# Two more column pairs of a decoder trunk with shared forms of x, further split pairs, and splits kept in order

## The chip, the cores and the metric

The kernel runs on one core of one Trainium2 chip. The metric is device time in microseconds (us), the median of the runs shown. The core's engines go by the profile's short names: PE (TensorE's matrix multiplications), PEld (its weight loads), DVE (VectorE), ACT (ScalarE), POOL (GpSimd) and SP (SyncE, which here only issues DMAs). Each engine works through a queue of its own in a fixed order and waits for the others by semaphores.

## The reference

One layer of a hybrid decoder for 256 tokens and a model width of 2048. All is float32.

```python
h = rmsnorm(x, norm_mix_g)
u = h @ w_in                     # 2048 x 12288
c_g, b_g, xa, za, q, fl, iv, og, ga, gb = split(u)   # 8 fields of 1024 columns, 2 of 2048
ya = b_g * causal_dwconv3(c_g * xa, conv_w) * silu(za)
o  = hgrn2_chunked(silu(q), (1 - lb) * sigmoid(-fl), iv, log_f(fl))   # gated recurrence, 8 heads of 128
yb = rmsnorm_per_head(o) * hg_norm_g * silu(og)
m  = sigmoid(ga) * (ya @ w_a_out) + sigmoid(gb) * (yb @ w_b_out)
x  = x + m @ w_o
x  = x + sigmoid(rmsnorm(x, ple_norm_g) @ w_ple_gate) * (p @ w_ple_proj)
return rmsnorm(x, final_norm_g)
```

## The kernel before

**Products.** Each float32 operand is split into a rounded high part and the rest: ACT writes the high part (`whi`, L154), DVE subtracts it from the operand for the low part (`wlo`, L155). A product of 128 rows by 128 tokens by 512 columns is then three matmuls: high by high, high by low, low by high. The norm's gain is folded into the transposed x when that is split (`put`, L258); the norm's factor for each token (`rstd1`) is applied when a result leaves PSUM.

**Groups and steps.** The columns of each weight are cut into groups of 512, and a group into chunks of 256 rows; a chunk is one step of the main loop. The groups follow one another: four for p (`PP`), then the fields of `w_in` in `IN_ORDER` (L37): for each half j of 512 columns f, q, iv, og, c, xa, za, b, then the gates with A (`w_a_out`) and B (`w_b_out`), then O (`w_o`) and PG (`w_ple_gate`). An ordinary step has 12 matmuls: two parts of 128 rows, two halves of 128 tokens, three matmuls each. The result lies in two PSUM banks, one for each half of the tokens.

**Pairs.** Three groups "GG" take the columns of a gate ga and a gate gb together, and "GP" two of the last gate's, in an order written out as a program (`GATES`, `LATE`, L42). An entry (g, c) is two ordinary steps of group g. An entry ("S", c) is the same chunk of both groups at once: a scheme with 7 in place of 8 products, in four steps of 2, 1, 2 and 2 products (`pair_products`, L1166). It needs combinations of the four weight blocks, made in place by DVE (`combine_weights`, L162 to L170: one operation of 1024 columns, two of 512, with a new tile `t2`), and four combinations of x, its forms (`forms`, L729, fed by `forms_of_x`, L750, which loads x anew). Its products are added into banks named 1, 5, 6, 7 (tag "s") and (0, 0), (1, 0), (0, 1) (tag "g", a half of the tokens and a group of the pair); `sums` (L773) adds these up, with one ACT copy and seven DVE additions, as soon as they are complete. The four steps split the weights as ordinary steps do, the second one half of a tile.

**Banks.** PSUM has eight banks here, four with the tag "g" and four with "s" (`bank`, L89). A bank that is asked for while its four are in use waits until one has been read.

**What goes ahead.** At each step the loop first splits the weights for the steps up to `ahead(pos)` in front (`ahead`, L1147; the loop at L1228): three, and one more around the GG groups. The split pairs lie in four buffers of the pool `wp`; around the GG groups one more pair in `tmp2` takes every fifth step (`more`, L214; `MORE`, L209). Weights come in units of two chunks, 1 MB, into three buffers `raw` (`load`, L103); `ask_ahead` (L1158) asks for them on SP's queue, in that queue's order with all other transfers.

**Epilogues.** What is done with a result is a generator; `advance` lets each active one do its next part after a step, behind the last splits (`step`, L1129, through `issue_after`, which sets the order in an engine's queue). Some results are turned by way of DRAM (`turned`, L292): four stores, a load, a 32 by 32 transposition on DVE. When the kernel is built, instructions get their places in the engines' queues by an assumed duration of each, with program order as the priority.

**Around the change.** Step 4 is f's first (half 0). At steps 10 to 13 x is loaded by tokens (`load_tokens`, L1042), at 13 to 16 ACT sums its squares (L1050), at 16 the norm's factor follows (`norm_of_x`, L1054: DVE, then POOL at L278), and at step 17 `ep_f` (L348) begins: ACT reads f's two banks (`scaled`, L315). Until then f keeps these two banks. q follows at step 12 and iv at step 20. `ep_q` (L399) makes q times its sigmoid and turns it, `ep_iv` (L405) scales the value, `ep_og` (L411) makes the output gate and then runs the recurrence (`hgrn`, L419), whose tiles X, a, both, aoff, y lie in `tmp1` and, for part of X, in the place of `ybT`. Temporaries of 4 KB a partition come from eight buffers (`t4`, L85).

Of the kernel before, what the change touches and what calls it, by code (L numbers as in the profile page):

```python
# [15 lines left out]
P = 128  # L16
# [7 lines left out]
CW = 512  # L24
# [17 lines left out]
GATES = ("S", 0), (0, 2), ("S", 1), (1, 2), ("S", 4), (0, 6), ("S", 5), (1, 6)  # L42
LATE = (0, 4), ("S", 0), (0, 6), ("S", 1), (2, 3), ("S", 2), (1, 4), (1, 6)
# [8 lines left out]
def hybrid_kernel(ctx, tc, xT, x, pT, prm, gfin, masks, w_in, w_a, w_b, w_o, w_pg, w_pp, out):  # L52
# [80 lines left out]
    def split(pos, c0=0, c1=2 * CW):  # L133
# [9 lines left out]
        if more(pos) and pos % (4 + MORE) < MORE:  # L143
            pool, n = pools[more(pos)], MORE
        if pos not in parts:
            parts[pos] = tuple(
                pool.tile([P, 2 * CW], F32R, tag=tag, bufs=n, name=nm(tag)) for tag in ("whi", "wlo")
            )
        hi, lo = parts[pos]
        s = slice(c0, c1)  # L150
        with ExitStack() as order:
            for i in state["before"].pop() if state.get("before") else ():
                order.enter_context(tc.issue_after(i))
# [8 lines left out]
    def combine_weights(pos):  # L162

        b = load(pos).rearrange("p i (k c) -> p (i k) c", k=2)
        t2 = half[unit_of[pos]] = pools["tmp2" if pos in gates else "tmp3"].tile([P, CW], F32, tag="t2", bufs=2 if pos in gates else 1, name=nm("t2"))
# [8 lines left out]
    for n, (kind, j) in enumerate(IN_ORDER):  # L174
        if j == 0 or kind not in ("ga", "gb"):
# [33 lines left out]
    LEAD, MORE = 3, 1  # L209
    of_kind = lambda *kinds: [pos for pos, (gi, c) in enumerate(steps) if groups[gi][0] in kinds]  # L210
    gates, late = of_kind("GG"), of_kind("PG")[0]
    gates = range(gates[0] - 12, gates[-1] + 9)

    def more(pos):  # L214

        return "tmp2" if pos in gates else None

    TOKENS, NORM = 10, 13
# [186 lines left out]
    def ep_iv(j, psum):  # L405
        v = t4("v", 1)
# [322 lines left out]
    def forms(op, pool, tag, r, chunks):  # L729
# [12 lines left out]
        hi, lo = (pool.tile([P, 4 * n * P], F32R, tag=tag + x, bufs=1, name=nm(tag + x)) for x in "hl")  # L742
# [7 lines left out]
    def forms_of_x():  # L750

        joined = sorted(c for u, c in GATES if u == "S")
        for n in range(0, len(joined), 2):
# [11 lines left out]
            yield from forms("hT", pools["tmp2"], f"Sx{n}", r, chunks)  # L765
# [35 lines left out]
    def ep_pair(j, e, left):  # L801
# [12 lines left out]
        yield from sums(e, left, tiles_of, then)  # L814

# [28 lines left out]
    def ep_o(j, psum):  # L844
# [18 lines left out]
        if j < 2:  # L863
# [9 lines left out]
            yield from forms("x1T", pools["tmp3"], f"So{j}", r, chunks)  # L873
# [273 lines left out]
    def ahead(pos):  # L1147

        return LEAD + min(max(pos - late - 4, 0) // 3, 5) + MORE * (more(pos + LEAD) is not None and more(pos + LEAD + MORE) == more(pos + LEAD))
# [67 lines left out]
    for pos, (gi, c) in enumerate(steps[:last_group]):  # L1217
# [26 lines left out]
        if pos == 4:  # L1244
            begin()
        if 0 <= pos - NORM < 4:
# [7 lines left out]
        if program:  # L1254
# [4 lines left out]
            if c == (min(n for n, (u, _) in enumerate(program) if u == "S"), 0):  # L1259
                active.append({"GG": ep_pair, "GP": ep_gates_late}[kind](j, banks, left))  # L1260
            pair_products(c, program, opname)
            ask_ahead()
            if not joint[pos] or c[1] % 2:
# [150 lines left out]
```

## Time and profile before

| | |
|---|---|
| runs, us | 814.44, 814.02, 814.43; median 814.43 |
| profiled execution | 814.02 us, of which the profile's span is 812.2 |
| mean granted TensorE clock | 0.996 |
| PE busy | 802.9 us, 4199 matmuls |
| PEld busy | 667.5 us |
| DVE busy | 625.9 us, 737 instructions |
| ACT busy | 463.5 us, 607 instructions |
| POOL busy | 91.1 us |
| DMA | 188.33 MB, mean 232 GB/s |

A matmul's record overlaps that of the next, so PE's busy time is how long at least one was under way, and the pace is read from the starts. In a list of groups the two numbers behind the bar are the busy time of the group in us and the mean of one in ns, and behind the next bar stands the idle time of the engine just ahead of these instructions with what ended it. In a timeline or a chain the first number is the start, the second the time it took.

### The profile page before, as it was taken

To read this page: it belongs to the slowest core of one execution; us is meant where nothing else is said; L and a number is where in the kernel's file an instruction comes from. 1 tells how busy PE (TensorE), PEld (TensorE's weight loads), DVE (VectorE), ACT (ScalarE), POOL (GpSimd) and SP (SyncE) were. 2 spreads that over 40 slices of the span, in tenths; PEclk is the share of its full clock that TensorE was granted. 3 is DMA by queue.
4 is the path that set the end of the run, shared out by engine and by line. 5 is a ranking of instruction groups with operands and counts; after the bars stand their busy time and mean duration, and the time that the engine had idled before them with its cause. 6 is when DMAs were issued, how large, how long until landed. Compare 5 with 4: busy or idle time off the path is not lost.

```text
span 812.2 us, 10984 instructions
## 1 busy us (share of the span) xinstructions
PE 802.9 (99%) x4199; PEld 667.5 (82%) x4199; DVE 625.9 (77%) x737; ACT 463.5 (57%) x607; POOL 91.1 (11%) x74
## 2 busy tenths in 40 slices
PE   9999999999999999999999999999999999999995
PEld 7888888888888888888888888888888888888885
DVE  5747697967766488967767998998997657679895
ACT  7667465555555465565664554564564456665652
POOL 1000045400000055200001000100100000002012
PEclk9999999999999999999999999999999999999998
DMA  9979656747767555647764774774866687887542
GB/s 339 372 276 342 224 170 208 230 167 238 257 234 255 184 185 201 214 155 261 271 239 146 225 268 148 250 258 157 259 230 230 215 304 245 295 301 270 201 144 105
DMA packets 46565, 188.33 MB, mean 232 GB/s; under 512 B 5296, under 2 KB 14768, under 8 KB 31408
## 3 DMA queue, kind: packets, MB, share of 16 engines
q1 hardware_dynamic: 46368, 187.36, 67.5%
q8 instruction: 33, 0.54, 0.3%
q10 hardware_dynamic: 144, 0.26, 0.1%
q14 instruction: 20, 0.16, 0.1%
HBM read 173.97 MB, written 13.63 MB: 231 GB/s over the span
## 4 chain that ended last, share of the span: by engine, by line
PE 88%; DVE 5%; DMA 3%; ACT 1%; issue 1%; SPq 0%; POOL 0%; ACTq 0%; POOLq 0%; DVEq 0%
PE g L1156 70%; PE g L1178 11%; PE s L1178 4%; DMA raw<-in_w_pg 2%; DVE wlo L155 2%; PE s L1156 1%; PE s L457 1%; ACT whi L154 1%; DVE raw L166 1%; DMA raw<-in_w_pp 0%; DVE t L920 0%; DVE xs L921 0%; DMA turn<-t 0%; DVE t L169 0%; DVE t L938 0%
## 5 line engine op out<-in xcount | busy, mean ns | idle before, releaser
L155 DVE TENSOR_TENSOR wlo<-raw,whi 128x1024 fp32r<-128x1024 f32 (+1 forms) x310 | 384.4, 1255 | 156.3 <-ACT whi L154 154.9
L154 ACT ACTIVATE whi<-raw 128x1024 fp32r<-128x1024 f32 (+1 forms) x310 | 320.0, 1049 | 250.7 <-PE g L1156 197.4
L1156 PE MATMUL g<-wlo,xh 128*128 128x512 f32 (+1 forms) x656 | 251.9, 384 | 0.0
L1156 PE MATMUL g<-whi,xl 128*128 128x512 f32 (+1 forms) x656 | 251.7, 384 | 0.0
L1156 PE MATMUL g<-whi,xh 128*128 128x512 f32 (+1 forms) x656 | 251.6, 385 | 0.0
L1156 PEld LDWEIGHTS g<-whi,xh 128*128 128x128 f32 x656 | 123.3, 188 | 24.5
L1156 PEld LDWEIGHTS g<-whi,xl 128*128 128x128 f32 x656 | 123.3, 188 | 24.5
L1156 PEld LDWEIGHTS g<-wlo,xh 128*128 128x128 f32 x656 | 123.3, 188 | 24.0
L1178 PE MATMUL g<-wlo,xh 128*128 128x512 f32 x166 | 64.6, 389 | 0.0
L1178 PE MATMUL g<-whi,xl 128*128 128x512 f32 x166 | 64.6, 389 | 0.0
L1178 PE MATMUL g<-whi,xh 128*128 128x512 f32 x166 | 64.4, 389 | 0.0
L1156 PE MATMUL g<-whi,mh 128*128 128x512 f32 x128 | 49.8, 389 | 0.0
L1156 PE MATMUL g<-wlo,mh 128*128 128x512 f32 x128 | 49.8, 389 | 0.0
L1156 PE MATMUL g<-whi,ml 128*128 128x512 f32 x128 | 49.6, 389 | 0.0
L154 ACT ACTIVATE whi<-t 128x512 fp32r<-128x512 f32 x15 | 9.5, 632 | 54.4 <-DVE t L169 54.4
L1178 PEld LDWEIGHTS g<-whi,xl 128*128 128x128 f32 x166 | 31.2, 188 | 6.5
L1178 PEld LDWEIGHTS g<-whi,xh 128*128 128x128 f32 x166 | 31.2, 188 | 6.5
L1178 PEld LDWEIGHTS g<-wlo,xh 128*128 128x128 f32 x166 | 31.1, 188 | 6.4
L832 POOL TENSOR_TENSOR t<-ga,gb 128x512 f32<-128x512 f32 x6 | 10.6, 1786 | 192.9 <-issue 118.1
L1156 PEld LDWEIGHTS g<-whi,ml 128*128 128x128 f32 x128 | 24.0, 188 | 5.0
L1156 PEld LDWEIGHTS g<-wlo,mh 128*128 128x128 f32 x128 | 24.0, 188 | 5.0
L1156 PE MATMUL g<-whi,yaTh 128*128 128x512 f32 (+1 forms) x74 | 28.0, 385 | 0.1
(250 smaller groups left out, 919.8 us busy)
## 6 DMA issues: line engine op xcount, KB each, us to landing
raw<-in_w_in SPq DMA_DIRECT2D x73, 1024.0 KB, 5.0
raw<-in_w_in SPq DMA_DIRECT2D x34, 512.0 KB, 6.6
raw<-in_w_o SPq DMA_DIRECT2D x16, 1024.0 KB, 6.0
raw<-in_w_pg SPq DMA_DIRECT2D x12, 1024.0 KB, 6.4
turn<-t SPq DMA_DIRECT2D x72, 128.0 KB, 2.7
t<-turn SPq DMA_DIRECT2D x18, 512.0 KB, 5.4
raw<-in_w_a SPq DMA_DIRECT2D x8, 1024.0 KB, 5.2
raw<-in_w_b SPq DMA_DIRECT2D x8, 1024.0 KB, 5.3
```

The lines of the kernel that those rows point to most:

```text
L154: a = nc.scalar.activation(out=hi[:, s], in_=src[:, s], func=AF.Copy)
L155: v = nc.vector.tensor_tensor(out=lo[:, s], in0=src[:, s], in1=hi[:, s].bitcast(F32), op=ALU.subtract)
L166: nc.vector.tensor_tensor(out=b[:, 0:4:3, :], in0=b[:, 0:3:2, :], in1=b[:, 3:4, :].to_broadcast([P, 2, CW]), op=ALU.subtract)
L457: nc.tensor.matmul(heads(bk)[r, h, c if at is None else slice(at, at + 32)], key(h)[:, r], query(h)[:, c], start=True, stop=True, tile_pos ...
L832: (nc.vector if j == 3 else nc.gpsimd).tensor_tensor(out=spread(m, t), in0=blocks(ga[:, s]), in1=blocks(gb[:, s]), op=ALU.add)
L1156: nc.tensor.matmul(psum, a, b, start=first and n == 0, stop=last and n == 2)
L1178: nc.tensor.matmul(banks[name], x, y[:, s], start=k == total[name] and i == 0, stop=k == 1 and i == 2)
```

## The change

q and iv of half 0 become one pair ("QV"), iv and og of half 1 another ("VG"). Both follow a new program, `INNER`: two ordinary entries of the first group, an S, one more of the first group, an S, then three of the second group. So half 0 has f, QV, og, c and so on, and half 1 f, q, VG, c. A new epilogue `ep_inner` adds the banks up by `sums` and hands the two results, now in SBUF, to the epilogues that they had before; `ep_iv` scales in place.

The forms of x for chunks 0 and 1 are made for these pairs too, from a load at step 9 (`FORMS`), into the part of `yaT` that half 1 fills later. Around the two pairs three steps of seven have their split pair in other tiles: both buffers of X; a and y; the two later parts of `ybT`. There up to three more steps are split ahead. The tile `t2` lies in `both` or `aoff`. And every split in the kernel is put behind the split before it in the queues of ACT and DVE (`state["splits"]`).

```diff
--- before.py
+++ after.py
@@ -40,6 +40,7 @@
 
 
 GATES = ("S", 0), (0, 2), ("S", 1), (1, 2), ("S", 4), (0, 6), ("S", 5), (1, 6)
+INNER = (0, 2), (0, 4), ("S", 0), (0, 6), ("S", 1), (1, 2), (1, 4), (1, 6)
 LATE = (0, 4), ("S", 0), (0, 6), ("S", 1), (2, 3), ("S", 2), (1, 4), (1, 6)
 
 
@@ -140,16 +141,18 @@
                 src, c1 = half[unit_of[pos]], CW
 
         pool, n = (pools["late"], 6) if (pos - state.get("late", len(steps))) % 10 < 6 and "late" in state else (wp, 4)
-        if more(pos) and pos % (4 + MORE) < MORE:
-            pool, n = pools[more(pos)], MORE
+        places = [(pool, n, tag) for tag in ("whi", "wlo")]
+        n = len(MORE[more(pos)])
+        if pos % (4 + n) < n:
+            places = [(pools[name], 1 + (tag == "X"), tag) for name, tag in MORE[more(pos)][pos % (4 + n)]]
         if pos not in parts:
             parts[pos] = tuple(
-                pool.tile([P, 2 * CW], F32R, tag=tag, bufs=n, name=nm(tag)) for tag in ("whi", "wlo")
+                pool.tile([P, 2 * CW], F32R, tag=tag, bufs=n, name=nm("w" + x)) for (pool, n, tag), x in zip(places, ("hi", "lo"))
             )
         hi, lo = parts[pos]
         s = slice(c0, c1)
         with ExitStack() as order:
-            for i in state["before"].pop() if state.get("before") else ():
+            for i in (*state.get("splits", ()), *(state["before"].pop() if state.get("before") else ())):
                 order.enter_context(tc.issue_after(i))
             a = nc.scalar.activation(out=hi[:, s], in_=src[:, s], func=AF.Copy)
             v = nc.vector.tensor_tensor(
@@ -162,7 +165,10 @@
     def combine_weights(pos):
 
         b = load(pos).rearrange("p i (k c) -> p (i k) c", k=2)
-        t2 = half[unit_of[pos]] = pools["tmp2" if pos in gates else "tmp3"].tile([P, CW], F32, tag="t2", bufs=2 if pos in gates else 1, name=nm("t2"))
+        pool, tag, n = ("tmp2", "t2", 2) if pos in gates else ("tmp3", "t2", 1)
+        if more(pos) == "inner":
+            pool, tag, n = "tmp1", ("both", "aoff")[unit_of[pos] // 2 % 2], 1
+        t2 = half[unit_of[pos]] = pools[pool].tile([P, CW], F32, tag=tag, bufs=n, name=nm("t2"))
         nc.vector.tensor_tensor(
             out=b[:, 0:4:3, :], in0=b[:, 0:3:2, :], in1=b[:, 3:4, :].to_broadcast([P, 2, CW]), op=ALU.subtract
         )
@@ -172,7 +178,11 @@
     groups = []
     groups += [("PP", j, w_pp, j, "pT") for j in range(4)]
     for n, (kind, j) in enumerate(IN_ORDER):
-        if j == 0 or kind not in ("ga", "gb"):
+        if (kind, j) in (("q", 0), ("iv", 1)):
+            groups.append(("QV" if j == 0 else "VG", j, w_in, n, "hT", INNER))
+        elif (kind, j) in (("iv", 0), ("og", 1)):
+            continue
+        elif j == 0 or kind not in ("ga", "gb"):
             groups.append((kind, j, w_in, n, "hT"))
         elif kind == "ga":
             groups.append(("GG", j, w_in, n, "hT", GATES))
@@ -206,16 +216,25 @@
     last_group = len(steps) - w_pg.shape[2]
 
 
-    LEAD, MORE = 3, 1
+
+    LEAD = 3
+    MORE = {
+        None: (), "gates": ((("tmp2", "whi"), ("tmp2", "wlo")),),
+        "inner": (
+            (("tmp1", "X"), ("tmp1", "X")), (("tmp1", "a"), ("tmp1", "y")), (("branch", "ybTh1"), ("branch", "ybTl1")),
+        ),
+    }
     of_kind = lambda *kinds: [pos for pos, (gi, c) in enumerate(steps) if groups[gi][0] in kinds]
     gates, late = of_kind("GG"), of_kind("PG")[0]
     gates = range(gates[0] - 12, gates[-1] + 9)
+    inner = [of_kind(kind) for kind in ("QV", "VG")]
+    inner = range(inner[0][0] - 3, inner[0][-1] + 1), range(inner[1][0] - 6, inner[1][-1] + 1)
 
     def more(pos):
 
-        return "tmp2" if pos in gates else None
-
-    TOKENS, NORM = 10, 13
+        return "gates" if pos in gates else "inner" if any(pos in at for at in inner) else None
+
+    TOKENS, NORM, FORMS = 10, 13, 9
     FIRST = 6
 
     praw = t4()[:, : 2 * T]
@@ -402,8 +421,8 @@
         plain_times(psum, sg, qt)
         state["qT", j] = yield from turned(qt, 5, t4("qT", 1))
 
-    def ep_iv(j, psum):
-        v = t4("v", 1)
+    def ep_iv(j, psum, v=None):
+        v = t4("v", 1) if v is None else v
         scaled(psum, v)
         state["v", j] = v
         yield
@@ -726,7 +745,7 @@
         yield
 
 
-    def forms(op, pool, tag, r, chunks):
+    def forms(op, made, r, chunks):
 
 
         n = len(chunks)
@@ -739,7 +758,7 @@
         nc.vector.tensor_tensor(out=s3, in0=a11, in1=a21, op=ALU.subtract)
         nc.vector.tensor_tensor(out=s4, in0=a12, in1=s2, op=ALU.subtract)
         yield
-        hi, lo = (pool.tile([P, 4 * n * P], F32R, tag=tag + x, bufs=1, name=nm(tag + x)) for x in "hl")
+        hi, lo = made()
         nc.scalar.activation(out=hi, in_=f, func=AF.Copy)
         nc.vector.tensor_tensor(out=lo, in0=f, in1=hi.bitcast(F32), op=ALU.subtract)
         for u in range(n):
@@ -747,9 +766,13 @@
                 s = slice((n * i + u) * P, (n * i + u + 1) * P)
                 state["S", op, chunks[u], i] = hi[:, s], lo[:, s]
 
-    def forms_of_x():
-
-        joined = sorted(c for u, c in GATES if u == "S")
+    def form_tiles(pool, tag, n=2):
+
+        return lambda: tuple(pool.tile([P, 4 * n * P], F32R, tag=tag + x, bufs=1, name=nm(tag + x)) for x in "hl")
+
+    def forms_of_x(program, made):
+
+        joined = sorted(c for u, c in program if u == "S")
         for n in range(0, len(joined), 2):
             chunks = joined[n : n + 2]
             raw = t4()
@@ -762,7 +785,7 @@
                     h = r[:, u, k, :]
                     nc.scalar.activation(out=h, in_=h, func=AF.Identity, scale=gain(PRM_GMIX, 2 * chunks[u] + k))
             yield
-            yield from forms("hT", pools["tmp2"], f"Sx{n}", r, chunks)
+            yield from forms("hT", made(n), r, chunks)
             yield
 
     def add(out, x, y):
@@ -812,6 +835,16 @@
                 )
 
         yield from sums(e, left, tiles_of, then)
+
+    def ep_inner(j, e, left):
+
+        def then(q, g):
+            halves = [g[:, A], g[:, B]]
+            after = ep_iv(j, halves, g) if q != j else (ep_og if j else ep_q)(j, halves)
+            next(after)
+            active.append(after)
+
+        yield from sums(e, left, lambda: (t4("v", 1), t4()) if j else (t4(), t4("v", 1)), then)
 
     def ep_a(j, psum):
         g = state["ga", j]
@@ -870,7 +903,7 @@
             yield
             chunks = [c for u, c in LATE if u == "S" and c // 2 == j]
             r = x1.rearrange("p (u k t) -> p u k t", u=2, k=2)[:, : len(chunks)]
-            yield from forms("x1T", pools["tmp3"], f"So{j}", r, chunks)
+            yield from forms("x1T", form_tiles(pools["tmp3"], f"So{j}", len(chunks)), r, chunks)
             return
         for c in range(4):
             put(state["x1T"], j * 4 + c, x1[:, c * T : (c + 1) * T], gain(PRM_GPLE, j * 4 + c))
@@ -1146,7 +1179,10 @@
 
     def ahead(pos):
 
-        return LEAD + min(max(pos - late - 4, 0) // 3, 5) + MORE * (more(pos + LEAD) is not None and more(pos + LEAD + MORE) == more(pos + LEAD))
+        at, n = more(pos + LEAD), 0
+        while n < len(MORE[at]) and more(pos + LEAD + n + 1) == at and (at == "gates" or more(pos + LEAD - 2 * n) == at):
+            n += 1
+        return LEAD + min(max(pos - late - 4, 0) // 3, 5) + n
 
     def product(psum, op, k, t, hi, lo, first, last, which=(0, 1, 2)):
 
@@ -1243,6 +1279,10 @@
             load_x(pos + 2)
         if pos == 4:
             begin()
+        if pos == FORMS:
+            held = [x[:, 4:, :].rearrange("p k t -> p (k t)") for x in state["yaT"]]
+            active.append(forms_of_x(INNER, lambda n: lambda: held))
+            step(active[-1])
         if 0 <= pos - NORM < 4:
             add_squares(pos - NORM)
         if pos == NORM + 3:
@@ -1257,9 +1297,11 @@
                 total = products_of(program)
                 left, banks = dict(total), {}
             if c == (min(n for n, (u, _) in enumerate(program) if u == "S"), 0):
-                active.append({"GG": ep_pair, "GP": ep_gates_late}[kind](j, banks, left))
+                active.append({"GG": ep_pair, "GP": ep_gates_late, "QV": ep_inner, "VG": ep_inner}[kind](j, banks, left))
             pair_products(c, program, opname)
             ask_ahead()
+            if 0 <= pos - TOKENS < 4:
+                load_tokens(pos - TOKENS)
             if not joint[pos] or c[1] % 2:
                 advance()
             if kind == "GP" and c in ((1, 1), (3, 1)):
@@ -1304,7 +1346,7 @@
             if kind == "ga" and j == 0:
                 finish()
                 second_part()
-                active.append(forms_of_x())
+                active.append(forms_of_x(GATES, lambda n: form_tiles(pools["tmp2"], f"Sx{n}")))
                 step(active[-1])
             if kind == "O" and j == 0:
                 state["x1T"] = operand(big, "x", KT)
```

## The prediction, made before the result was known

> **What bounds the kernel now.** I read the page first: the busy times, then the slices.
>
> ```profile
> span 812.2 us, 10984 instructions
> ...
> PE 802.9 (99%) x4199; PEld 667.5 (82%) x4199; DVE 625.9 (77%) x737; ACT 463.5 (57%) x607; POOL 91.1 (11%) x74
> ...
> PE   9999999999999999999999999999999999999995
> ...
> PEclk9999999999999999999999999999999999999998
> DMA  9979656747767555647764774774866687887542
> ```
>
> PE is busy in every slice but the last, at full clock. DVE comes next with 77%, and DMA is nearly full in the first four slices, some 80 us. Busy alone doesn't say that PE is never late, so I went to the chain of work that ended last, whose PE pieces give the true pace:
>
> ```profile
> 16.36 119.68 PE g L1156 x528
> ...
> 178.21 138.73 PE g L1156 x612
> ```
>
> 119.68/528 and 138.73/612 are both 0.2267 us a matmul: stretches of 120 us and more without a hole. The 384 ns that the page gives as the mean of one overlap their neighbours, so a matmul that goes away is worth 0.2267 us, not 0.384. The forecast has one main term then: how many matmuls go. And one question: does PE stay as dense?
>
> The Trainium skill, "TensorE: Matmul & The Clock Gate", section "Back-to-back issue gap", gives about 131 ns sustained for 512 columns; by that twelve matmuls would be an estimated 1.6 us. The trace shows 0.2267 us here, and it decides.
>
> **The change part by part.**
>
> *Matmuls removed.* A plain unit of two chunks takes 2 x 12 matmuls, and a joint unit ("S") of four steps 6+3+6+6 = 21. Each program of INNER has two S units, and two pairs use it: 4 x 3 = 12 matmuls go, 12 x 0.2267 = **2.72 us**. They lie in stretches where PE is dense, so all of it counts if nothing stalls. Nothing else leaves PE.
>
> *Vector and scalar work added.* From the groups by line:
>
> ```profile
> L155 DVE TENSOR_TENSOR wlo<-raw,whi 128x1024 fp32r<-128x1024 f32 (+1 forms) x310 | 384.4, 1255 | 156.3 <-ACT whi L154 154.9
> L154 ACT ACTIVATE whi<-raw 128x1024 fp32r<-128x1024 f32 (+1 forms) x310 | 320.0, 1049 | 250.7 <-PE g L1156 197.4 <-issue 13.8 <-DMA raw<-in_w_pg 12.3
> L166 DVE TENSOR_TENSOR raw<-raw 128x1024 f32<-128x1024 f32 x15 | 19.3, 1289 | 0.4
> L169 DVE TENSOR_TENSOR t<-raw 128x512 f32<-128x512 f32 x15 | 11.4, 757 | 0.5
> L170 DVE TENSOR_TENSOR raw<-raw,t 128x512 f32<-128x512 f32 x15 | 10.4, 692 | 0.5
> L155 DVE TENSOR_TENSOR wlo<-t,whi 128x512 fp32r<-128x512 f32 x15 | 10.4, 691 | 0.7
> L769 DVE TENSOR_TENSOR gb<-gb,s 128x512 f32<-128x512 f32 (+1 forms) x9 | 7.7, 861 | 0.0
> L769 DVE TENSOR_TENSOR ga<-gb,g 128x512 f32<-128x512 f32 x6 | 4.1, 682 | 0.0
> L769 DVE TENSOR_TENSOR gb<-gb,g 128x512 f32<-128x512 f32 x6 | 3.8, 684 | 0.0
> ```
>
> An S unit costs DVE 3 x 1.255 + 0.691 + 1.289 + 0.757 + 0.692 = 7.2 us where a plain unit costs 2.5: +4.7, four times 18.8. The sums of a pair are a third of the three L769 groups, (7.7+4.1+3.8)/3 = 5.2, twice 10.4. The forms of x once: about 1.6 for four quarter-size operations, an estimate from the 0.69 of half-size ones, and 1.25 for the low part, which has the shape of a full split. Together 32 us, so DVE goes from 626 to about 658 of 810 us (81%). ACT gets some 11 us (four full and four half splits are 6.3 by its row; the rest copies and the scaling of x). None is on PE's path while splits are made ahead. In an S unit DVE needs 7.2 us against 21 x 0.2267 = 4.8 of PE, so the lead must be there beforehand: over one program DVE's splits take 6 x 2.5 + 2 x 7.2 = 29.4 us and PE 186 x 0.2267 = 42.2. The three added split pairs let splits run six steps ahead instead of three: up to 16 us of cover in plain steps, against a deficit of 2.4 us an S unit. If the cover were gone, those 2.4 us would be the price of each. The windows say where DVE has room:
>
> ```profile
> 27.00:38.00 11.00, 11.00 (x51) 9.09 (x50) 8.47 (x12) 5.64 (x7) 0.00 (x0) 1.00 1.01 378
> 38.00:49.00 11.00, 11.00 (x50) 9.13 (x49) 4.91 (x4) 5.28 (x6) 0.00 (x0) 1.00 1.03 412
> 60.00:71.00 11.00, 11.00 (x50) 9.13 (x49) 7.34 (x7) 6.08 (x8) 0.00 (x0) 1.00 0.99 305
> 71.00:82.00 11.00, 11.00 (x50) 9.09 (x50) 8.81 (x14) 9.97 (x13) 0.00 (x0) 1.00 0.95 359
> 257.00:268.00 11.00, 11.00 (x50) 9.13 (x49) 5.81 (x5) 5.50 (x6) 0.00 (x0) 1.00 0.54 179
> ```
>
> (Columns: the stretch and its length, then busy PE, PEld, DVE, ACT, POOL with counts, the clock, DMA share, GB/s.) The second pair, around 240 to 284 us, has half of DVE and DMA free: I cost it at nothing beyond its gain of 1.36 us. The query's sums, gates and turned copy end some 5 us later than now, but their reader, the recurrence, starts after og at 103 us, 20 us on.
>
> *DMA added and moved.* Two loads of 256 KB of x at step 9, about 30 us in, on the full DMA: 0.52 MB at 378 to 412 GB/s is 1.3 us of delay for what queues behind on SP: weights, then the four loads of x by tokens. The weight loads are asked for as far ahead as the splits, so three steps earlier against the turned copies, for which SP stands still; that helps and is costed at nothing.
>
> *The bank that the first pair needs earlier.* Only four banks have the tag "g". The first group, f0, holds two until its eviction at L315, since that needs the norm of x, which needs the tokens:
>
> ```profile
> L1046 SPq DMA_DIRECT2D t<-in_x x4: 328/380/496, 33.9 to 41.3; - x4
> ...
> DMA to landing us min/median/max: 8.4/9.9/10.2
> ```
>
> ```profile
> 55.44 1.04 ACT L1050 ACTIVATE t<-t 128x1024 f32<-128x1024 f32 x1
> ...
> 57.90 1.27 ACT L315 ACTIVATE t<-g,r1r 128x512 f32<-128x512 f32 x2 [1.32 <-POOL r1r L278]
> ```
>
> ```profile
> 59.71 0.39 PE L1156 MATMUL g<-whi,xh 128*128 128x512 f32 x1
> ```
>
> The first eviction ends at 57.90 + 0.69 = 58.6, the second at 59.2; the value's first matmul, at 59.71, takes the fifth bank: half a microsecond to spare. In the changed kernel the fifth bank is (0, 1), first written in the last part of the first S unit. The query starts at 16.36 + 96 x 0.2267 = 38.1; four plain steps and 15 matmuls later is 38.1 + 63 x 0.2267 = **52.4 us**. The eviction cannot be that early: the last token load, issued at 41.3, lands by 51.5 at the latest and then 1.3 later, at 52.8; from the last square's start to the first eviction's end it takes 58.6 - 55.44 = 3.15. So the bank is free at 55.9 at the earliest, 3.5 us after PE would want it. Unmoved it is 6.2; with the squares behind the second S unit's combinations on DVE (2.7 us more) 8.9. That is the unknown of this change: 0 to 8.9.
>
> What lies beside that wait is other matmuls. The matmuls' order is fixed when the kernel is built, and the trace shows that it isn't always the program's:
>
> ```profile
> 734.32 0.61 PE L1178 MATMUL g<-whi,xh 128*128 128x512 f32 x2
> ...
> 736.13 0.39 PE L1156 MATMUL g<-whi,xh 128*128 128x512 f32 x1
> ...
> 737.04 0.39 PE L1178 MATMUL g<-whi,xl 128*128 128x512 f32 x1
> ```
>
> Here the gate's first group (L1156) lacks its last part of x1, and matmuls of the next pair (L1178) stand in between, without a hole. In the same way three matmuls of the S unit (0.7 us) and the 24 of (0, 6) on banks already held (5.4 us) can go ahead of bank (0, 1): 6.1 us, about the 6.2 needed. What stands behind a matmul that waits is all of PE, so what isn't covered counts in full. I take the wait as nearly hidden: 0.1 by these numbers, **0.3 us** with some allowance. The ends stay 0 and 8.9 less what is filled.
>
> *Splits in order of use; other buffers.* Each split is put behind the one before it on ACT and DVE. With a shared order nothing is issued more. It can lose where a split waits for its buffer ahead of one that needn't. ACT's largest wait in its row above is for PE's release, which comes in order of use as well: 0, within plus or minus 0.5. The tiles borrowed for splits (X, a, y and others) are first written by the recurrence about a step after the pair ends: 0.
>
> *Sum.* The profiled execution took 814.02 us (span 812.2 and 1.8 around it). 814.02 - 2.72 + 0.3 = 811.6. The runs shown have a median of 814.43, 0.4 above it; I go half way: **811.8**.
>
> **The rivals.**
>
> *Part of the wait stays.* The order is fixed before, by assumed durations; where norm and eviction come later on the chip than assumed, PE stands. The chain from the last square to the eviction crosses four engines, which speaks for it. 2 us left, a third of the 6.2, gives 814.02 - 2.72 + 2 = 813.3. The same place and size would fit the forms of x, or the first S unit's splits, coming late.
>
> *The wait stays whole (the other side).* If no matmul is put ahead, PE stands from 52.4 to about 58.6: 814.02 - 2.72 + 6.2 = 817.5. It turns slower than before when more than 2.7 us stay uncovered. For it speaks that the program has (0, 1) first; against it the interleaving above. A clock drop could follow:
>
> ```profile
> 800.00:805.00 5.00, 3.79 (x32) 3.59 (x30) 3.52 (x12) 2.17 (x4) 0.62 (x2) 1.00 0.55 210
> 805.00:812.00 7.00, 0.00 (x0) 0.00 (x0) 2.14 (x6) 1.33 (x2) 0.54 (x1) 0.57 0.39 150
> ```
>
> PE's last work ends at 803.8; a mean of 0.57 over 7 us is full clock for 1 us and half for 6, so it fell 2.2 us after. How soon it returns no row shows: between 0 and the 6 us seen, at half pace 0 to 3 us, so up to 820.5. The Trainium skill, "TensorE: Matmul & The Clock Gate", section "Part 1: The HAM clock gate", says that an idle window of about 3.4 us halves the clock and a busy one restores it; by that an estimated 1.7 us are added, 819.2. The trace agrees on the halving.
>
> *DVE becomes the bound from 60 to 80 us.* f0's chain and the query's share it there with the pair's splits and sums; rows above show 7.34 and 8.81 of 11 busy, and the pair adds 4.7 + 5.2 us. That is 26 of 22, the rest before and after. If the lead is used up, the 4 us appear: 815.3. Splits come first in order, which speaks against it.
>
> **How the numbers follow.** Forecast, wait hidden to within 1.4 us, 811.3 to 812.8: 0.57. Partial wait or DVE's bound, 812.8 to 816: 0.18. Whole wait, 816 to 820.5: 0.25. About 0.2% (1.6 us) is what a measurement of this kernel can tell from no change, so faster is 0.57, same 0.18, slower 0.25. The range goes from 810.9 (0.4 of spread under 811.3) up to 817.5, which takes in the lower part of the whole wait and leaves out a little under 2 in 10.
>
> **What would show it.** Right: twelve matmuls fewer, no PE hole near 52 to 60 us, and in that stretch matmuls of the plain steps ahead of bank (0, 1)'s; from the end of the first pair everything 1.4 us earlier, from the second 2.7; the last square near 54 to 56 us. Wrong: a PE idle row whose releaser is L315, or a clock under 1.00 near 55 us (the whole wait); ended by L155 after 60 us (DVE); holes elsewhere (order of splits). A time under 810.9 would mean that something beside matmuls got shorter.

## The result, and the profile after

| | before | after |
|---|---|---|
| median of 6 runs each, us | 814.24 (814.02 to 814.44) | 816.84 (816.24 to 819.55) |
| ratio | | 1.0037, 95% interval 1.0027 to 1.0047 |
| profiled execution, its span | 814.02, 812.2 | 817.8, 815.7 |

The change makes the kernel slower by 0.37%. The forecast was 811.8, faster. The profiled execution of the changed kernel, 817.8, lies 1.0 above its median, so what its stages lose adds up to more than the 2.6 between the medians. The page of the changed kernel, the lines that answer to those of before:

```profile
span 815.7 us, 11029 instructions
...
PE 803.3 (98%) x4186; PEld 666.5 (82%) x4187; DVE 650.0 (80%) x776; ACT 471.2 (58%) x622; POOL 87.1 (11%) x74
...
PE   9999899999999999999999999999999999999995
...
PEclk9999999999999999999999999999999999999998
DMA  9988645656775835656774774764765787886542
```

One digit of PE's row has become an 8: the fifth slice, 81.6 to 102 us. DVE has 24 us more work where I had 32, and is busy for 80%. Of PE's waits by what ended them, one row stands outside the kernel's first microseconds:

```profile
PE g L1192 <- DVE wlo L158: 2.7, 2, 2.4
```

(Microseconds in all, times, the longest. L1192 is the product of an ordinary step, L1156 before; L158 is the split, L155 before.) To find what each stage won or lost I took the start of each group's first matmul from both timelines:

| group's first matmul | before | after | difference |
|---|---|---|---|
| f, half 0 | 16.19 | 16.73 | +0.54 |
| q, now the first pair | 37.95 | 38.49 | +0.54 |
| og, half 0 | 81.47 | 81.24 | -0.24 |
| c, half 0 | 103.23 | 107.28 | +4.05 |
| q, half 1 | 218.87 | 222.88 | +4.01 |
| c, half 1 (behind the second pair) | 284.15 | 286.80 | +2.65 |
| last group | 781.24 | 783.89 | +2.65 |
| end of the last matmul | 803.79 | 807.10 | +3.31 |

The first pair wins 1.36 and loses 0.58 in small holes; the output gate behind it loses 4.29; the second pair wins 1.36 whole; the last group loses 0.66. The 0.54 at the start is not the change's: in the profiles of the experiments below, PE's first product starts anywhere from 5.10 to 5.60 us, in kernels with and without the pairs.

The 4.29 us, PE's timeline (start, duration, and in brackets the idle time and its releaser):

```profile
81.24 0.61 PE L1192 MATMUL g<-whi,xh 128*128 128x512 f32 x2
84.22 0.78 PE L1192 MATMUL g<-wlo,xh 128*128 128x512 f32 x1 [2.37 <-DVE wlo L158]
...
86.93 0.63 PE L1192 MATMUL g<-whi,xl 128*128 128x512 f32 x1
87.36 0.55 PE L1192 MATMUL g<-whi,xh 128*128 128x512 f32 x1
87.75 0.39 PE L1192 MATMUL g<-wlo,xh 128*128 128x512 f32 x1
```

From one matmul's start to the next 2.75 us pass, 2.5 more than a matmul's 0.2267. Then the matmuls start 0.43 us apart until 87.4 us: the clock was halved. The windows show it (stretch, length, busy PE, PEld, DVE, ACT, POOL, then the clock):

```profile
80.85:84.26 3.41, 1.04 (x6) 0.54 (x4) 3.41 (x8) 3.38 (x5) 0.00 (x0) 1.00 0.49 121
84.26:87.68 3.42, 3.42 (x8) 2.74 (x9) 3.42 (x3) 0.00 (x0) 0.10 (x1) 0.50 0.56 133
87.68:91.09 3.41, 3.41 (x16) 2.76 (x16) 3.41 (x7) 2.29 (x3) 1.92 (x1) 1.00 0.97 400
```

So 2.5 us of the 4.29 are the hole, and the other 1.8 are the clock's.

**Why the split was late.** DVE's timeline up to it:

```profile
71.14 1.25 DVE L326 STREAM_TRANSPOSE t<-t 128x1024 f32<-128x1024 f32 x1 [1.43 <-DMA t<-turn]
74.80 2.36 DVE L158 TENSOR_TENSOR wlo<-raw,whi 128x1024 fp32r<-128x1024 f32 x2 [2.41 <-ACT whi L157]
77.08 0.68 DVE L792 TENSOR_TENSOR v<-v,s 128x512 f32<-128x512 f32 x1
77.67 0.41 DVE L379 TENSOR_SCALAR t<-t,lc,lc 128x256 f32<-128x256 f32 x1
78.00 0.68 DVE L792 TENSOR_TENSOR t<-v,g 128x512 f32<-128x512 f32 x1
78.59 1.05 DVE L379 TENSOR_SCALAR t<-t,lc,lc 128x256 f32<-128x256 f32 x3
79.56 1.21 DVE L792 TENSOR_TENSOR v<-v,s 128x1024 f32<-128x1024 f32 x1
80.69 1.29 DVE L359 TENSOR_TENSOR t<-t,t 128x512 f32<-128x512 f32 x2
81.90 1.13 DVE L386 TENSOR_SCALAR kT<-t,lc 128x256 f32<-128x256 f32 x4
82.95 2.35 DVE L158 TENSOR_TENSOR wlo<-raw,whi 128x1024 fp32r<-128x1024 f32 x2
```

DVE is idle for 3.84 us first (1.43 waiting for f's turned copy, 2.41 for a high part), and then does the pair's sums (L792), the query's product (L359) and f's scaling (L379, L386) in one heap. The split for the output gate's first step (at 82.95) stands behind all of it. Before, it was the second of the two in this row; it began at 77.11 and was done 3.1 us ahead of the first product of its step at 81.47:

```profile
75.98 2.35 DVE L155 TENSOR_TENSOR wlo<-raw,whi 128x1024 fp32r<-128x1024 f32 x2
```

What DVE waited for stands on SP's queue (start, the issue's duration), first after, then before:

```profile
61.67 1.78 SPq L320 DMA_DIRECT2D turn<-t  x4
63.50 0.45 SPq L1293 DMA_DIRECT2D mask_t<-in_masks  x1
66.10 0.34 SPq L322 DMA_DIRECT2D t<-turn  x1
66.54 10.97 SPq L122 DMA_DIRECT2D raw<-in_w_in  x4
```

```profile
46.80 0.43 SPq L1253 DMA_DIRECT2D mask_t<-in_masks  x1
```

```profile
61.07 0.89 SPq L119 DMA_DIRECT2D raw<-in_w_in  x2
63.79 0.33 SPq L303 DMA_DIRECT2D t<-turn  x1
```

Before, two weight loads went out between the stores and the load of f's turned copy, and the masks had been loaded 14 us ahead. After, the masks took the place of the weights, SP stood for the stores until 66.1, and the weights came behind it: ACT's next high part started at 73.70, when the first of them had landed.

### The profile page after: what moved, and what is told of

It reads as the page before. It is cut to its first block, busy times and chain, and to the rows that moved or that the text cites. A ratio compares the mean times of both kernels' runs of the same rounds, so it can differ in the third digit from the quotient of the medians.

```text
span 815.7 us, 11029 instructions
## 1 busy us (share of the span) xinstructions
PE 803.3 (98%) x4186; PEld 666.5 (82%) x4187; DVE 650.0 (80%) x776; ACT 471.2 (58%) x622; POOL 87.1 (11%) x74
## 4 chain that ended last, share of the span: by engine, by line
PE 87%; DVE 6%; DMA 3%; ACT 2%; issue 2%; POOL 0%; SPq 0%; ACTq 0%; POOLq 0%; DVEq 0%
PE g L1192 62%; PE g L1214 17%; PE s L1214 5%; DVE wlo L158 2%; DMA raw<-in_w_pg 1%; DMA raw<-in_w_in 1%; ACT whi L157 1%; PE s L1192 1%; PE s L476 1%; PE s L1067 1%; DVE raw L172 0%; DVE t L953 0%; DVE xs L954 0%; DMA turn<-t 0%; ACT t L1083 0%
## 5 line engine op out<-in xcount | busy, mean ns | idle before, releaser
L158 DVE TENSOR_TENSOR wlo<-raw,whi 128x1024 fp32r<-128x1024 f32 (+1 forms) x314 | 388.1, 1258 | 130.9 <-ACT whi L157 128.9
L1192 PE MATMUL g<-wlo,xh 128*128 128x512 f32 (+1 forms) x528 | 203.0, 385 | 2.7 <-DVE wlo L158 2.7
L1192 PE MATMUL g<-whi,xh 128*128 128x512 f32 (+1 forms) x528 | 202.7, 385 | 0.0
L1192 PE MATMUL g<-whi,xl 128*128 128x512 f32 (+1 forms) x528 | 202.6, 384 | 0.0
L1192 PEld LDWEIGHTS g<-wlo,xh 128*128 128x128 f32 x528 | 99.8, 189 | 22.8 <-DVE wlo L158 3.6
L1192 PEld LDWEIGHTS g<-whi,xh 128*128 128x128 f32 x528 | 99.5, 188 | 19.6
L1192 PEld LDWEIGHTS g<-whi,xl 128*128 128x128 f32 x528 | 99.7, 189 | 19.4
L1214 PE MATMUL g<-wlo,xh 128*128 128x512 f32 x270 | 105.2, 389 | 0.0
L1214 PE MATMUL g<-whi,xl 128*128 128x512 f32 x270 | 105.1, 389 | 0.0
L1214 PE MATMUL g<-whi,xh 128*128 128x512 f32 x270 | 104.7, 390 | 0.0
L1214 PEld LDWEIGHTS g<-whi,xh 128*128 128x128 f32 x270 | 50.7, 188 | 11.0 <-ACT whi L157 0.4
L1214 PEld LDWEIGHTS g<-wlo,xh 128*128 128x128 f32 x270 | 50.7, 188 | 10.9 <-DVE wlo L158 0.3
L1214 PEld LDWEIGHTS g<-whi,xl 128*128 128x128 f32 x270 | 50.7, 188 | 10.4
L1192 PE MATMUL g<-whi,mh 128*128 128x512 f32 x128 | 49.8, 389 | 0.0
L1192 PE MATMUL g<-wlo,mh 128*128 128x512 f32 x128 | 49.8, 389 | 0.0
L1192 PE MATMUL g<-whi,ml 128*128 128x512 f32 x128 | 49.6, 389 | 0.0
L1192 PEld LDWEIGHTS g<-whi,mh 128*128 128x128 f32 x128 | 24.0, 188 | 5.0
L1192 PEld LDWEIGHTS g<-whi,ml 128*128 128x128 f32 x128 | 24.0, 188 | 5.0
L1192 PE MATMUL g<-whi,yaTh 128*128 128x512 f32 (+1 forms) x74 | 28.1, 386 | 0.0
```

The lines of the kernel that those rows point to most:

```text
L158: v = nc.vector.tensor_tensor(out=lo[:, s], in0=src[:, s], in1=hi[:, s].bitcast(F32), op=ALU.subtract)
L1192: nc.tensor.matmul(psum, a, b, start=first and n == 0, stop=last and n == 2)
L1214: nc.tensor.matmul(banks[name], x, y[:, s], start=k == total[name] and i == 0, stop=k == 1 and i == 2)
```

## The experiments

The median of the kernel before was 814.28 to 814.60 beside these kernels (814.38 beside 1 to 4, 814.33 beside 5 to 8, 814.60 beside 9 to 11, 814.28 beside 12), so kernels of different rounds are best compared by what each is above or below it.

| kernel | median, us | ratio to before, 95% interval |
|---|---|---|
| 1 second pair alone | 815.92 | 1.0018 (1.0009 to 1.0026) |
| 2 first pair alone | 818.43 | 1.0061 (1.0049 to 1.0073) |
| 3 both, splits without an order | 816.54 | 1.0026 (1.0016 to 1.0035) |
| 4 both, longer lead | 814.45 | 1.0001 (0.9992 to 1.0009) |
| 5 before, with the order alone | 815.79 | 1.0013 (1.0004 to 1.0022) |
| 6 second pair alone, no order | 815.73 | 1.0016 (1.0007 to 1.0025) |
| 7 longer lead, masks later | 813.52 | 0.9992 (0.9983 to 1.0001) |
| 8 longer lead, masks later, no order | 812.14 | 0.9971 (0.9959 to 0.9982) |
| 9 as 6, the cycle moved by four | 813.89 | 0.9992 (0.9984 to 1.0001) |
| 10 before, order up to PG | 814.55 | 0.9998 (0.9990 to 1.0007) |
| 11 both, masks later | 814.86 | 0.9998 (0.9987 to 1.0008) |
| 12 as 8, order up to PG | 812.13 | 0.9974 (0.9962 to 0.9985) |

**1. The second pair alone.**

```diff
-        if (kind, j) in (("q", 0), ("iv", 1)):
+        if (kind, j) == ("iv", 1):
...
-        elif (kind, j) in (("iv", 0), ("og", 1)):
+        elif (kind, j) == ("og", 1):
...
-    inner = range(inner[0][0] - 3, inner[0][-1] + 1), range(inner[1][0] - 6, inner[1][-1] + 1)
+    inner = (range(inner[0] - 6, inner[-1] + 1),)
```

> Only the second pair (value and output gate of the second half) is made; query and value of the first half are plain groups again; the split order, the forms' load at step 9 and all else stay. Two theories. T1, the tail of the first pair: the loss of the changed kernel is made in one place, where the output gate of the first half waits at 81.5 us for its first split on DVE, and the halved clock behind it. T2, the order of splits: putting every split behind the one before it costs over the whole kernel, the late start of PE and the hole at 793.4 us with it. T1: the second pair's 6 matmuls of 0.2267 us go and nothing is lost, 814.24 - 1.36 = 812.9, at most 0.8 more if start and end keep what they lost. T2: the start's 0.5 and the end's 0.75 stay, 814.1, and holes beside.

Measured: 815.92. Both theories missed. The wait at 81.5 us is gone, and the pair wins its 1.36 (c of half 1 goes from +0.88 to -0.49). But the profile has two holes that neither kernel has: 0.9 us with its next step at 349.7 us, 1.0 us at 647 to 650 us. Experiments 6 and 9 go on with them.

**2. The first pair alone**, the same edit for the other pair.

> Only the first pair is made; value and output gate of the second half are plain groups again. T1: the wait at 81.5 us and the slow clock behind it stay whole, the second pair's 1.36 us are missing: 816.84 + 1.36 = 818.2. T2, the order of splits: the same 818.2. A third theory, T3, that both pairs lose a little: below 817.5.

Measured: 818.43. The wait is there (2.73 us from start to start at 81.2 us), the clock behind it is halved for 3.41 us, and the output gate loses 4.24. So the loss belongs to the first pair. The sum is right partly by chance: this kernel, with one pair, has the hole at 651 us as well (0.86).

**3. Splits without an order.**

```diff
-            for i in (*state.get("splits", ()), *(state["before"].pop() if state.get("before") else ())):
+            for i in state["before"].pop() if state.get("before") else ():
```

> Both pairs; the splits are no longer put behind one another in the queues of ACT and DVE. T1: the output gate's first split is late because of what stands ahead of it on DVE and because of its lead, not because of the order among splits: the hole at 81.5 us stays within 0.7 us, 816.8 (816.0 to 817.6). T2: the hole shrinks or goes, and with it the slow clock, 812.5; or start and end get their 1.25 us back, 815.6.

Measured: 816.54. The hole stays (2.80 us from start to start at 82.9 us): T1. There is none near 790 us any more. The output gate loses 2.7 here and not 4.3, as the clock did not fall:

```profile
80.57:83.98 3.41, 2.73 (x13) 1.92 (x11) 3.41 (x8) 3.38 (x6) 0.00 (x0) 1.00 0.64 264
83.98:87.40 3.42, 1.68 (x7) 1.42 (x8) 3.42 (x6) 1.76 (x3) 0.00 (x0) 1.00 0.66 153
```

The hole is as long as before, but lies across two of these stretches, with PE busy for 2.73 us of one and 1.68 of the other. What that saves is lost ahead of it: the first pair wins 1.36 and loses 2.07 here, in holes at 61 to 65 and at 77 us, where the changed kernel loses 0.58.

**4. A longer lead.**

```diff
-    inner = range(inner[0][0] - 3, inner[0][-1] + 1), range(inner[1][0] - 6, inner[1][-1] + 1)
+    inner = range(inner[0][0] - 3, inner[0][-1] + 8), range(inner[1][0] - 6, inner[1][-1] + 1)
```

> The range of steps in which splits have the three added pairs of tiles is made seven steps longer at the first pair's end, so that splits go six steps ahead through the output gate's steps too; no operation is added or taken away. T1a, the lead that falls from 6 to 3 at the pair's end puts the output gate's first split behind the query's product, the sums and f's scaling on DVE: now it stands ahead of some 4 us of them, the hole of 2.5 us goes and the 1.8 us of halved clock with it, 816.84 - 4.3 = 812.5. T1b, DVE has simply too much to do from 75 to 88 us whatever the order: the hole comes back at a later step, 815 or more.

Measured: 814.45, which is 2.4 us less than the changed kernel: between the two expectations, nearer to T1b's number. The profile, of an execution of 815.99, shows what is left. DVE:

```profile
80.30 1.22 DVE L158 TENSOR_TENSOR wlo<-raw,whi 128x1024 fp32r<-128x1024 f32 x1
...
83.77 1.14 DVE L386 TENSOR_SCALAR kT<-t,lc 128x256 f32<-128x256 f32 x4
84.82 4.62 DVE L158 TENSOR_TENSOR wlo<-raw,whi 128x1024 fp32r<-128x1024 f32 x4
```

The output gate's first split now stands ahead of the query's product and f's last scaling and comes 2.65 us earlier. The second stands behind them, and PE waits for it, 0.8 us and with the clock full. This profile has also lost 1.56 us in the last group, which experiments 5 and 10 explain.

**5. The order of splits alone**, the edit of the change's `for` line put into the kernel before.

> The kernel before with one edit alone: every split is put behind the split before it on ACT and DVE. It changes the places of a few splits among one another, near the second joint unit of two GG pairs and in the last gate's pair. T2 (the order of splits costs): 815.6, with holes of PE in the last group or before the O groups as the profiles with this order show. T1 (the loss is the first pair's tail alone): 814.4, within 0.5.

Measured: 815.79, so T2 is right on this term: 1.46 us. That is a median between two heaps: five of the eleven executions take 814.3 to 814.6, like the kernel before, and six take 815.8 to 816.7. By these heaps the order costs some 2 us in about half of the executions and next to nothing in the others. In the profile, of 816.25, all that is lost lies in the last group but for 0.5 at the start. DVE's timeline of before, and then of this kernel:

```profile
744.85 3.49 DVE L155 TENSOR_TENSOR wlo<-raw,whi 128x1024 fp32r<-128x1024 f32 x3
748.37 2.19 DVE L166 TENSOR_TENSOR raw<-raw 128x1024 f32<-128x1024 f32 x1
```

```profile
745.28 6.82 DVE L155 TENSOR_TENSOR wlo<-raw,whi 128x1024 fp32r<-128x1024 f32 x4
752.14 1.23 DVE L166 TENSOR_TENSOR raw<-raw 128x1024 f32<-128x1024 f32 x1
```

With the order a fourth split has to be done before the joint unit's combination (L166) can start, 3.8 us later than before where PE is 0.5 later. The next weight loads go out 2.5 us later (758.41 against 755.90), and the last group's splits come behind:

```profile
792.67 0.50 PE L1156 MATMUL g<-wlo,xh 128*128 128x512 f32 x1 [0.57 <-DVE wlo L155]
```

**6. The second pair alone, no order**, the edits of 1 and 3.

> The second pair alone, as in the first experiment, but the splits not put behind one another. That experiment gave 815.9 where 812.9 was expected, with a late start and two holes of 1.0 us at 350 and 647 us. If the order of splits made them: 813.0 to 813.5. If not, 815.9 again: then it is the four steps more, which shift the cycle of five in which the GG pairs' extra split tiles are used, or the forms' load.

Measured: 815.73. The order is not what made the single pair's holes: that at 349 us and those at 648 to 650 us are still there, and two more stand at 265 and 268 us. That the medians of 1 and 6 agree doesn't show that the order costs nothing: experiment 1 has two heaps as well, 814.5 to 815.1 (five executions) and 815.9 to 817.3 (six), and its profile, of 815.11, is one of the lower and loses nothing in the last group. Without the order there is one heap, 815.1 to 816.6.

**7. Longer lead and the masks later.**

```diff
+        if pos == NORM + 21:
             nc.sync.dma_start(out=mask_t, in_=masks)
```

(with the lead's edit of 4; the load leaves step 17, `NORM + 4`).

> The long lead of the fourth experiment, and the load of the masks moved from step 17 to step 34. There it stood on SP's queue between the stores of f's turned copy and its load, and the weight loads behind both. If f's late chain on SP is what crowds DVE and ACT from 72 us on, the turned copy and the weights land some 1.7 us earlier, the remaining holes at 76 (0.5) and 84.9 us (1.1) go: 814.45 - 1.6 = 812.9 (812.3 to 813.4). If DVE's work alone sets it, 814.4 again.

Measured: 813.52, 0.9 less than 4 where 1.6 was expected. In the profile both holes are gone, and the output gate takes what it took before (its start and that of c both stand at -0.25). The rest of the expectation is eaten by the last group, which loses 1.44.

**8. The same without the order.**

> As the run before, without the order among splits. If the order costs something in the last group (holes of 0.6 and 0.7 us near 790 us in the fourth experiment's profile): 0.5 to 1.3 us less than that run. If not, the same within 0.4.

Measured: 812.14, 1.4 less than 7 and 2.2 less than before (0.9971): the change's gain, at last. DVE does the same work (648.9 us), and the output gate's splits come in time:

```profile
77.11 1.21 DVE L158 TENSOR_TENSOR wlo<-raw,whi 128x1024 fp32r<-128x1024 f32 x1
...
81.63 4.62 DVE L158 TENSOR_TENSOR wlo<-raw,whi 128x1024 fp32r<-128x1024 f32 x4
```

The first is 5.84 us earlier than in the changed kernel. That refutes T1b: DVE hadn't too much to do, it had it too late. But little is left: from 71 to 92 us DVE is now busy for 20.5 of 21 us, where it was for 17.3 before the change, and PE is dense. PE's starts against before: -0.77 behind the first pair, -2.09 behind the second and to the end.

**9. The single pair with the cycle moved.**

```diff
-        if pos % (4 + n) < n:
-            places = [(pools[name], 1 + (tag == "X"), tag) for name, tag in MORE[more(pos)][pos % (4 + n)]]
+        if (pos + 4) % (4 + n) < n:
+            places = [(pools[name], 1 + (tag == "X"), tag) for name, tag in MORE[more(pos)][(pos + 4) % (4 + n)]]
```

> The second pair alone without the order among splits (815.73), and the cycles of five and seven steps in which split pairs take the extra tiles moved by four steps, so that they fall as they do with both pairs. On SP's queue this puts the stores and the load of a turned copy ahead of a weight load each near 635 us. If the cycle's phase makes the single pair's holes: those at 648 to 650 us (0.8) and at 264.7 and 268 us (0.8) go, 815.73 - 0.8 to 1.6 = 814.1 to 814.9; the hole at 350.6 us (0.7), which the profile puts down to no releaser, may stay. If it doesn't: 815.7.

Measured: 813.89, 1.84 less than 6, and 2.1 less when each is taken against the kernel before beside it. The holes at 265 to 268 and 648 to 650 us are gone, the one at 349 us stays (1.1 us from start to start, no releaser). SP's queue, in 6 and then in 9:

```profile
634.47 1.77 SPq L320 DMA_DIRECT2D turn<-t  x4
640.18 0.35 SPq L122 DMA_DIRECT2D raw<-in_w_o  x1
640.70 0.34 SPq L322 DMA_DIRECT2D t<-turn  x1
```

```profile
633.19 1.78 SPq L320 DMA_DIRECT2D turn<-t  x4
635.07 0.39 SPq L122 DMA_DIRECT2D raw<-in_w_o  x1
637.66 0.34 SPq L322 DMA_DIRECT2D t<-turn  x1
```

In 6 the weight load between stores and load has no free buffer until 640.18, and the turned copy, an operand of O, waits behind it. A pair has four steps more than its two groups, so with one pair the cycles stand four steps from where they stand with two, and the places with two are harmless here.

**10. Before, with the order up to the PG groups.**

```diff
-            for i in state["before"].pop() if state.get("before") else ():
+            for i in (*(state.get("splits", ()) if "late" not in state else ()), *(state["before"].pop() if state.get("before") else ())):
```

> The kernel before with the order among splits up to the PG groups and none from there on: only two splits each near two GG pairs change places. If the order costs in the last group alone, where a full split now stands behind the adding up of PG's result: 814.3, within 0.3, and no holes near 790 us. If it costs elsewhere: 815.8 as with the order everywhere.

Measured: 814.55 beside 814.60, and no hole after 360 us. In this kernel the order costs from PG on, and nowhere else. The spread points the same way: the seven kernels that keep the order to the end (the changed one, 1, 2, 4, 5, 7 and 11) have 2.4 to 4.3 us between their shortest and longest execution, the six others 0.7 to 2.3.

**11. The masks later, nothing else.**

> The changed kernel (lead and order as they are) with the load of the masks moved to step 34 and nothing else. T1 in its form of SP's queue: the turned copy of f and the weight loads behind it land 1.7 us earlier, so the wait of 2.5 us at 81.5 us shrinks to about 0.8, and with it the halved clock goes in most executions: 816.84 - 1.7 to 3.5 = 813.3 to 815.1. T1 in its form of the lead: the output gate's first split keeps its place behind the query's, the sums' and f's operations, and the wait stays over 2 us: 816.3 or more.

Measured: 814.86 (812.49 to 816.82), inside the first expectation. The output gate's first split starts at 81.49 instead of 82.95, the wait shrinks from 2.5 to 1.0, and the clock stays full. But it isn't f's turned copy that comes earlier, as expected:

```profile
64.09 0.35 SPq L122 DMA_DIRECT2D raw<-in_w_in  x1
66.18 0.34 SPq L322 DMA_DIRECT2D t<-turn  x1
```

Its load goes out as late as in the changed kernel (66.10). What has moved is one weight load, now ahead of it, and with that the split of those weights, at 70.99 in place of 74.80, in the time in which DVE had been idle. So the first pair's loss has two handles, the queue's order and the lead; taken against the kernel before beside each, the lead alone is worth 2.5 us (4) and the queue's order alone 2.3, and only with both has PE no hole over 0.2 us between 65 us and the last group (7, 8).

**12. As 8, with the order up to PG.**

> Both pairs, the long lead, the masks at step 34, and the order among splits kept up to the PG groups and dropped from there on. If the order costs in the last group alone, all of the gain of the eighth experiment is there: 812.1, within 0.4, about 2.2 us under the kernel before. If the order is worth something in the first pair, less than 811.8; if it costs there too, 812.6 or more.

Measured: 812.13, the same as 8. This is the change whole, but for the lead's seven steps, the masks' place and the order in the last part, and it beats both kernels: 0.9974 (0.9962 to 0.9985) of before. In its profile, which is of its longest execution (813.58), PE loses 1.3 us at 61 to 65 us to a high part and to the bank:

```profile
62.57 0.50 PE L1214 MATMUL g<-whi,yaTh 128*128 128x512 f32 x1 [0.23 <-ACT t L334]
```

## Why the prediction was wrong

*Matmuls removed, 2.72 us: right.* The second pair wins its 1.36 whole; the first wins 0.95 at best (8), for 0.4 of small holes at 63 us.

*The bank of the first pair, 0.3 us: right, but partly by luck.* It was the part I held for the risk of this change. In the changed kernel the eviction is later still, and PE hardly notices:

```profile
60.38 1.27 ACT L334 ACTIVATE t<-g,r1r 128x512 f32<-128x512 f32 x2 [0.28 <-POOL r1r L297]
```

```profile
49.00:60.00 11.00, 11.00 (x50) 9.12 (x49) 7.89 (x13) 7.65 (x12) 0.37 (x1) 1.00 0.74 304
```

PE is dense through the 11 us in which I had put the wait of 3.5 to 8.9 us; at 53 to 57 us it does the matmuls of (0, 6) ahead of the bank's. Both numbers under the 0.3 were too small. The first eviction ends at 61.07, 8.3 us after the place of the bank's first product in program order (38.49 + 63 x 0.2267 = 52.77); I had counted on 6.2. And that product stands at 61.38, behind 101 matmuls and not 63, so 8.6 us of others went ahead of it where I had 6.1. Behind it come small holes, 0.36 together, at 63 us, for which the profile names no releaser. The profiles of experiments 3 and 12 name the eviction, with 0.2 us each. The last square, forecast at 54 to 56 us, came at 58.02.

*DVE's 32 us "none on PE's path while splits are made ahead": the step that failed.* The cover was counted where it is largest, six steps, and the demand over 22 us as a mean. But the extra pairs of tiles end with the pair, so the lead falls from six to three just where its sums fall due. And the mean hid that DVE was idle for 3.84 us of that stretch: from 60 to 82 us it was busy for 16.8 of 22 us, and not for 26. The rival "DVE becomes the bound" had the place, 60 to 80 us; that "splits come first in order" I held against it, and the trace shows the split behind seven rows of sums, product and scaling. The size of 32 us isn't what failed: measured, it was 24.

*SP's queue, "that helps and is costed at nothing": failed too.* I priced the two added loads of x, 1.3 us, but not a change of the queue's order: the masks' load slid from 46.80 to 63.50, between the turned copy's stores and its load, and pushed the weights behind both. Moving that one load is worth 2.3 us (11). Why the planner put it there, no run shows.

*The clock.* A drop was in the text, but tied to the whole wait for the bank alone. A hole of 2.5 us was enough for it, so DVE's rival had 2.5 and 1.8 to lose. That is 4.3 where I wrote 4, by another working: the 4 were work that DVE couldn't place, and held nothing for the clock. That 816.84 lies inside the stated range, among the numbers that I gave to the whole wait for the bank (816 to 820.5), is chance: that wait didn't come.

*Splits in order, 0 within 0.5: failed.* It costs 1.46 by the median, by the two heaps some 2 in about half of the executions, all from PG on (5, 10).

*Borrowed tiles, 0: right for the tiles.* What I did not see is that the places of the tiles go by the step's number, which the pairs shift; it cost about 2 us where one pair stands alone (6, 9). With two pairs, no hole of that kind is seen.

*The second pair, no cost: right.* It won its 1.36 in the changed kernel.

What stays open: the hole at 349 us with a single pair, which has no releaser in the profile; and why taking the order away from the changed kernel alone won only 0.3 us (3) where it won 1.4 behind the two other edits (7, 8). Its profile says as much as this: the last group lost nothing and the clock didn't fall, but the holes at 61 to 65 and at 77 us took 1.5 more than in the changed kernel. Holes like those at 61 to 65 us come in experiment 12's longest execution too, with the order kept there, so they may go by execution and not by the order.

## What to carry to other kernels

A mean share of an engine says little about a change that adds work at one place: list what falls due there in the order of that engine's queue, and ask what lead is left at the very end of the stretch, where the extra buffers stop. When a step gets later, look for the transfers that the planner will now put in between: a load that is needed 40 us later can stand in front of the one that is needed now. And an edit that "only" fixes an order, or shifts a step's number under a modulo, deserves a run of its own.

## What the runs showed of the hardware

The granted clock is decided in stretches of 3.413 us. By the trace's clock records of the changed kernel it rose at 5.756 and fell at 84.263, 23.0 times 3.413 later, and came back after one; in the third experiment it fell 236.0 times 3.413 after it rose. A hole of 2.75 us halved it where PE was busy for 1.04 us of one stretch, a hole of 2.80 us did not where two stretches kept 2.73 and 1.68 us of work. So nearly the same wait cost 4.3 us in one execution and 2.7 in the other, as it fell. In which executions it falls how, no run shows but those profiled, so how much of the spread of the times this makes stays open.

The end of the kernels bears it out. The kernel before has its last matmul end at 803.79 and its clock fall at 805.99, 235.0 times 3.413 after it rose, behind this stretch:

```profile
802.57:805.99 3.42, 1.22 (x11) 1.02 (x9) 2.40 (x11) 0.47 (x1) 0.55 (x1) 1.00 0.46 181
```

Counted so in all fourteen traces, the clock fell sixteen times, each time behind a stretch with PE busy for 1.22 us or less, and it fell behind none with 1.68 us or more. Where between the two the limit lies, these traces don't show.

The Trainium skill, "TensorE: Matmul & The Clock Gate", section "Part 1: The HAM clock gate", says that the window is free-running and 4096 cycles at 1.2 GHz long, 3413 ns. The trace agrees on that; it adds that a hole shorter than the window is enough.
